# A hybrid decoder layer: gate operand sums made on chip, and rotary queries ahead of the GLA output halves

## The chip, the core and the metric

The kernel runs on one core of a Trainium2 chip. The metric is the time of one execution on the device in microseconds (us); before the change its median is 903.59 us over three runs (901.25 to 905.59). The core has five engines with a queue of instructions each: TensorE (PE) multiplies into PSUM, VectorE (DVE) and ScalarE (ACT) do elementwise work, GpSimd (POOL) does elementwise work in SBUF, and SyncE (SP) issues transfers. POOL and ACT issue some transfers too. An engine takes its queue in order.

## The reference

One layer of a decoder, 512 tokens of width 1024, in float32. A first LayerNorm gives h. From h one input projection makes the inputs of two branches: gated linear attention (GLA, four heads) and multi-head latent attention (MLA, eight heads, with a query latent of 384 and a key-value latent of 256). Two sets of gates are made from h as well and merge the branches; the output projection, a residual with LayerNorm, a squared-ReLU MLP of width 4096 and a last LayerNorm follow:

```python
h = layer_norm(x, ln_in_g, ln_in_b)
q_g, k_g, v_g, r_g, a_lr, q_lat, kv_lat, gate_logits = split(h @ w_in)
o_gla = rms_norm(gla_chunked(q_g, k_g, v_g, log_a))
y_gla = (o_gla * silu(r_g)) @ w_o_gla
q     = rms_norm(q_lat) @ w_q_b          # per head 128 plain and 64 rotary
kv    = rms_norm(kv_lat[:256]) @ w_kv_b  # per head 128 keys, 128 values
y_mla = merge_heads(causal_attention(q, rope(q), kv, k_rope)) @ w_o_mla
g_gla, g_mla = split(sigmoid(gate_logits + b_gate))
h = layer_norm(alpha * h + (g_gla * y_gla + g_mla * y_mla) @ w_out)
h = layer_norm(alpha * h + square(relu(h @ w_ff1)) @ w_ff2)
```

## The kernel before, in words

**Split numbers.** A float32 operand is kept as two parts, a high one rounded to the format that TensorE multiplies fast (`fp32r`) and a low one with the rest. A product takes three matmuls: high by high, high by low, low by high. `split` makes the parts: ScalarE copies (line 111 or 114), VectorE subtracts (112 or 115). Of h the kernel keeps only its two parts, eight tiles `hT` of 128 x 2 x 512 (feature rows by part by token).

**Weights.** All weights come through one stream, a list of entries in the order in which the plan calls stand in the code. `plan` appends entries of two 128-row blocks; `pump` (line 162 on) issues the loads on SP's queue up to two entries ahead and the splits (L185 on ACT, L186 on DVE) one entry ahead. High and low parts have two buffers each, so the split of an entry waits until the entry two before it is used up. `gemm_fm` (feature rows out, L238 to L240) and `gemm_tm` (token rows out, L271 to L273) consume them; an entry of a 512-wide `gemm_fm` is 24 matmuls of 512 columns. Their accumulators come from a PSUM pool `mm` of four banks; a second pool `px` of four banks serves the attention work.

**Stages around the change.** The *head* (0 to about 45 us) loads x, normalises it and transposes it into hT (`ln_transpose`, L406 to L420), one half of the tokens after the other, while the latent projections run. It also stores the unsplit h, tile by tile in halves of 256 tokens, from POOL's queue into DRAM tiles `hrawd` (L420). Then come the GLA projections with the GLA level work of each head woven between (`gla_levels`, `gla_out`; L657 to L800). The *first half of the gates* is two plain `gemm_fm` of hT (loop over `mb`). The *second half* is a Strassen-like product (`gemm_unit`, L1000 on): seven half-size products named in `FMO` in the order 11, 21, t1, 22, t2, t3, t4, whose h-side operands include four sums and differences of quarter blocks of h. A generator `op_sums` makes these during the first half of the gates: it loads two row blocks of raw h from `hrawd` into a tile `hraw` (L970, SP, prefetched up to two pairs ahead), forms four combinations `X` on VectorE (L974 to L977), and splits them (`sh`).

After the gates stand, in this order: output half 0 of the GLA branch (`y_gla(0)`), the rotary queries of heads 0 to 3 (`mla_qr(0)`), projections and attention of heads 0 and 1 (`mla_pair(0)`), output half 1 of GLA (`y_gla(1)`), the rotary queries of heads 4 to 7 (`mla_qr(1)`), and the other three pairs of heads. `mla_qr` multiplies the query latents `qlT` (three tiles `latT`) by the rotary columns of `w_q_b`, four token blocks of 256 columns in two PSUM banks, then applies the rotation (L487 to L489 on DVE, L490 on POOL), scales and splits (L114, L115), and spawns a generator that transposes the result (L821) into `QS`. The latents had been stored to DRAM (L541) and are loaded again (L1080) by the function `after`, which runs behind each of the seven products.

**What sets the order.** Generators (GLA heads, attention heads, transposes, `h_sums`) are advanced by `tick`, called between the matmul groups of a running product, so the program's text is already a weave. The kernel is then built with a scheduler that, on a timeline of its own at build time, gives each engine the earliest ready instruction in program order; what comes out is a fixed order per engine. Tiles come from pools with fixed counts (24 buffers of tag A for most, 22 of tag B), and an instruction that needs a buffer waits for its release.

Of the kernel before, what the change touches and what calls it, by code (L numbers as in the profile page):

```python
# [10 lines left out]
F32 = mybir.dt.float32  # L11
# [5 lines left out]
ALU = mybir.AluOpType  # L17
AX = mybir.AxisListType

P = 128  # L20
T = 512
# [31 lines left out]
def tile_hybrid_block(ctx: ExitStack, tc: tile.TileContext, I, out, dbg=None):  # L53
    nc = tc.nc
# [18 lines left out]
    def A(shape, dt=F32, n="a"):  # L73
        tag, bufs = ("C", 8) if n in TAG_C else (n, TAG_W[n]) if n in TAG_W else ("A", 24)
        return pa.tile(shape, dt, tag=tag, bufs=bufs, name=nm(n))
# [7 lines left out]
    def DR(shape, n):  # L83
        n = nm(n)
        return pd.tile(shape, F32, tag=n, name=n)
# [7 lines left out]
    def f(ap):  # L93
        return ap.bitcast(F32)

    act = nc.scalar.activation
    vtt = nc.vector.tensor_tensor
# [45 lines left out]
    def plan(name, c0, n, k_lo=0, k_hi=None, heads=None, res=False, per=2):  # L143
        w = I[name]
        K = w.shape[0] // P
        k_hi = K if k_hi is None else k_hi
        idx = []
        for k0 in range(k_lo, k_hi, per):
            nk = min(per, k_hi - k0)
            if heads is None:  # L150
                src = w.rearrange("(k p) n -> p k n", p=P)
                dmas = [(slice(0, nk), src[:, k0:k0 + nk, c0:c0 + n], None)]
            else:
                hw, h0, nh = heads
                src = w.rearrange("(k p) (h c) -> p k h c", p=P, c=hw)
                cw = n // nh
                dmas = [(kk, src[:, k0 + kk, h0:h0 + nh, c0:c0 + cw], cw) for kk in range(nk)]
            idx.append(len(stream))
            stream.append({"dmas": dmas, "nk": nk, "n": n, "res": res})
        return {"idx": idx, "nk": k_hi - k_lo, "per": per}  # L160
# [64 lines left out]
    def part(x, i, c):  # L225
        return x[i][:, c] if isinstance(x, tuple) else x[:, i, c]
# [72 lines left out]
    def plan_qr(g):  # L299
        PL["qr", g] = plan("w_q_b", NOPE, 4 * ROPE, heads=(HQ, 4 * g, 4))  # L300
# [26 lines left out]
    for key in UNITS:  # L327
        PL[key] = []
        for op, _ in FMO:
            for hf in range(2):  # L330
                PL[key].append(len(stream))
                e = {"nk": 2, "n": T, "res": False}
                if op[0] != "t":
                    e["dmas"] = [(slice(0, 2), u_src(key, int(op[0]) - 1, int(op[1]) - 1, hf), None)]
                else:
                    e["src"] = lambda q=(key, (op, hf)): WQ[q]
                if op == "22":
                    e["post"] = lambda raw, q=(key, "t1", "t2", hf): u_sum(*q, raw)
                elif op == "t2":
                    e["post"] = lambda raw, q=(key, "t2", "t4", hf): u_sum(*q, WQ[key, ("21", q[3])])  # L340
                stream.append(e)
    PL["yg", 0] = plan("w_o_gla", 0, T)
    plan_qr(0)

    def plan_pair(pr):
        PL["qn", pr] = plan("w_q_b", 0, 2 * P, heads=(HQ, 2 * pr, 2))
        PL["kn", pr] = plan("w_kv_b", 0, 2 * P, heads=(2 * P, 2 * pr, 2))
        PL["mv", pr] = plan("w_kv_b", P, 2 * P, heads=(2 * P, 2 * pr, 2))

    plan_pair(0)  # L350
    PL["yg", 1] = plan("w_o_gla", T, T)
    plan_qr(1)
    plan_pair(1)
    plan_pair(2)
    plan_pair(3)
# [43 lines left out]
    def ln_transpose(rows, g, b, outs, hf, alt=False, n="h0"):  # L399
        tk = slice(hf * 256, (hf + 1) * 256)  # L400
        for k in range(NK):
            if len(outs) <= k:
                outs.append(A([P, 2, T], F32R, n) if n == "h0" else (B([P, T], F32R, n), B([P, T], F32R, n)))
            p = MM() if alt and k in (4, 5) else PX()
            for i in range(2):
                nc.tensor.transpose(p[:, i * P:(i + 1) * P], rows[2 * hf + i][:, k * P:(k + 1) * P], ident)  # L406
            tmp = B([P, 256], F32, "lnt")
            hi, lo = part(outs[k], 0, tk), part(outs[k], 1, tk)
            ha = act(hi, p[:, :256], AF.Identity, scale=g[:, k:k + 1], bias=b[:, k:k + 1])
            if alt and k % 2:  # L410
                act(tmp, p[:, :256], AF.Identity, scale=g[:, k:k + 1], bias=b[:, k:k + 1])
            else:
                vts(tmp, p[:, :256], g[:, k:k + 1], b[:, k:k + 1], op0=ALU.mult, op1=ALU.add)
            hd = vtt(lo, tmp, f(hi), op=ALU.subtract)
            if n == "h1":
                st["ln"] = (ha, hd)
            else:
                if len(rawd) <= k:
                    rawd.append(DR([P, T], "hrawd"))
                nc.gpsimd.dma_start(rawd[k][:, tk], tmp)  # L420
            yield hd

    mvin = consts.tile([P, NT, 2], F32, name="mvin")
    hT, rawd = [], []

    def ln_in0():
        for tt in range(2):
# [87 lines left out]
    qlT, ckT, qld, ckd, GL, KKs = [], [], [], [], [], []  # L515
# [286 lines left out]
    def mla_qr(g):  # L802
        qst = []

        def ev_qr(a, j, ps):
            src = ps[:, :4 * ROPE].rearrange("p (h c) -> p h c", c=ROPE)
            csb = cs2[:, a, None, :].to_broadcast([P, 4, ROPE])
            snb = sn2[:, a, None, :].to_broadcast([P, 4, ROPE])
            t1 = B([P, 4, ROPE], F32, "rt1")
            t2 = B([P, 4, ROPE], F32, "rt2")  # L810
            rope(src, csb, snb, t1, t1, t2)
            q2 = B([P, 4, 2, ROPE], F32R, "q2")
            split(t1, q2[:, :, 0, :], q2[:, :, 1, :], scale=scale)
            qst.append(q2)
        gemm_tm([PL["qr", g]], qlT, 4 * ROPE, ev_qr)

        def tr():
            for h in range(4):
                p = PX(dt=F32R)
                for tt in range(NT):  # L820
                    nc.tensor.transpose(p[:, tt * P:(tt + 1) * P], qst[tt][:, h].rearrange("p a b -> p (a b)"), identr)  # L821
                yield
                q = B([P, T], F32R, "QS")
                act(q, f(p), AF.Copy)
                QS[4 * g + h] = q
        return spawn(tr())
# [134 lines left out]
    t_gla = [t_lv, t_out]  # L961


    def op_sums(srcs, rest, new, ops):
        raws = []
        for p in range(4):
            while len(raws) < min(4, p + 2):
                raws.append(A([P, 2, T], F32, "hraw"))
                for i in range(2):
                    nc.sync.dma_start(raws[-1][:, i], rest[2 * len(raws) - 2 + i])  # L970
            raw = raws[p]
            a11, a12, a21, a22 = raw[:, 0, :256], raw[:, 1, :256], raw[:, 0, 256:], raw[:, 1, 256:]
            X = A([P, 4, 256], F32, "hx")
            vtt(X[:, 0], a21, a22, op=ALU.subtract)  # L974
            vtt(X[:, 1], X[:, 0], a11, op=ALU.subtract)
            vtt(X[:, 2], a12, X[:, 1], op=ALU.add)
            vtt(X[:, 3], a11, a21, op=ALU.subtract)  # L977
            yield
            o = {0: (0, 0), 1: (1, 0), 4: (1, 1)}
            o = {ph: tuple(part(srcs[2 * p + i], w, slice(256 * h, 256 * h + 256)) for w in range(2))  # L980
                 for ph, (i, h) in o.items()}
            xs = new()
            for i in range(2):
                xh, xl = xs[i]
                split(X[:, 2 * i:2 * i + 2], xh, xl)
                o[(2, 5)[i]], o[(3, 6)[i]] = (xh[:, 0], xl[:, 0]), (xh[:, 1], xl[:, 1])
            yield
            ops.append(o)
# [8 lines left out]
    def gemm_unit(key, ops, evac, after=None):  # L997
# [3 lines left out]
        for n, (op, ph) in enumerate(FMO):  # L1001
# [43 lines left out]
            if after:  # L1045
                after(op)
# [13 lines left out]
    hops = []  # L1060

    def h_sums():
        yield from op_sums(hT, rawd,
                           lambda: [[B([P, 2, 256], F32R, "sh") for _ in range(2)] for _ in range(2)], hops)

    t_h = spawn(h_sums())
# [5 lines left out]
    def after(op):  # L1072
        if op == "11":
            u_load("g1", "t3")
            u_load("g1", "21")
        if op == "t4":
            for outs, rest in ((qlT, qld), (ckT, ckd)):
                for d in rest:
                    outs.append(A([P, 2, T], F32R, "latT"))
                    nc.sync.dma_start(f(outs[-1]), d)  # L1080
    gemm_unit("g1", hops, ev_gate, after)
    hT = hops = None


    def y_gla(mb):
        def ev_y(a, ps):
            g = gt[mb * 4 + a]
            stt(g[:, 0, :], g[:, 0, :], 1.0, ps, op0=ALU.add, op1=ALU.mult)
        gemm_fm(PL["yg", mb], ogT, T, ev_y)
# [17 lines left out]
            return omT[h]  # L1107
    omT_lazy = Lazy()

    WID[0] = 2  # L1110
    y_gla(0)
    mla_qr(0)
    WID[0] = 4
    t0, mv = mla_pair(0)
    mv()
    y_gla(1)
    mla_qr(1)
    t1, mv = mla_pair(1)
    mv(lambda: finish(*t0))
    t2, mv = mla_pair(2)  # L1120
# [283 lines left out]
```

## Time and profile before

| | |
|---|---|
| median of three runs | 903.59 us (901.25 to 905.59) |
| profiled execution | 902.01 us, span 900.2 us |
| granted TensorE clock | 0.998 |
| busy: TensorE, VectorE, ScalarE, GpSimd | 880.5, 580.5, 426.9, 181.1 us |
| transferred | 111.47 MB, mean 124 GB/s |

The profile is of one execution. "Busy" of TensorE counts matmuls from start to end, and neighbours overlap, so full busy time doesn't mean peak speed. A row of a group gives line, engine, operation, tiles (out<-in) and shapes, the number of instructions, and then busy time and mean duration or, in the view of a tile, the shortest, median and longest duration in ns and the first and last start in us. A row of the timeline begins with start and duration in us; what is in square brackets is the idle time of that engine just before it and what ended it. `xN` behind a row of the timeline stands for N like instructions in a row.

### The profile page before, as it was taken

The numbers are of one execution on the slowest core, as the hardware profiler recorded it, in microseconds if no ns is written. First come the engines' busy times: TensorE is split into PE (matmuls) and PEld (weight loads), VectorE is DVE, ScalarE is ACT, GpSimd is POOL, SyncE is SP. The second block draws the span as 40 slices with busy tenths as digits, with TensorE's granted clock in tenths as the row PEclk, the third lists the DMA queues.
The fourth block names the chain that finished last, engine by engine and source line by source line (L and its number), as shares of the span: only waits on it lengthen the run. The fifth ranks groups of instructions, "written<-read, shape, count | busy, mean of one in ns | idle before, by whom it ended". The sixth has DMA issues, their size and how long they took to land.

```text
span 900.2 us, 12222 instructions
## 1 busy us (share of the span) xinstructions
PE 880.5 (98%) x4652; PEld 755.2 (84%) x4652; DVE 580.5 (64%) x945; ACT 426.9 (47%) x729; POOL 181.1 (20%) x212
## 2 busy tenths in 40 slices
PE   5999999999999999999999999999999999999996
PEld 5988888888889988888888888988888888888885
DVE  7834855577956626576856797997557646723565
ACT  5556443444546524446644423366367546733410
POOL 3203442443511001010000002104400520142200
PEclk9999999999999999999999999999999999999999
DMA  7614423217326624112207618005941990494421
GB/s 260 198 47 156 129 67 94 71 47 215 113 71 211 188 59 126 27 54 65 82 24 271 197 47 304 1 0 151 296 115 32 260 246 24 116 204 110 132 67 74
DMA packets 66699, 111.47 MB, mean 124 GB/s; under 512 B 8225, under 2 KB 28065, under 8 KB 66641
## 3 DMA queue, kind: packets, MB, share of 16 engines
q1 hardware_dynamic: 52496, 77.67, 27.5%
q0 software_dynamic: 12224, 29.37, 13.7%
q10 hardware_dynamic: 1920, 3.66, 1.2%
q8 instruction: 36, 0.59, 0.3%
q14 instruction: 23, 0.18, 0.1%
HBM read 91.28 MB, written 6.82 MB: 109 GB/s over the span
## 4 chain that ended last, share of the span: by engine, by line
PE 95%; DVE 2%; DMA 2%; ACT 1%; issue 0%; SPq 0%; DVEq 0%; POOL 0%; ACTq 0%
PE mm L238 14%; PE mm L239 14%; PE mm L240 14%; PE mm L271 7%; PE mm L273 7%; PE mm L272 7%; PE px L1275 2%; PE px L1274 2%; PE px L1273 2%; PE px L727 2%; PE mm L1275 2%; PE mm L1274 2%; PE mm L1273 2%; PE mm L1023 1%; PE mm L1021 1%; PE mm L1022 1%
## 5 line engine op out<-in xcount | busy, mean ns | idle before, releaser
L186 DVE TENSOR_TENSOR wlo<-wraw,whi 128x1024 fp32r<-128x1024 f32 (+1 forms) x102 | 115.5, 1133 | 145.1 <-ACT whi L185 141.0
L185 ACT ACTIVATE whi<-wraw 128x1024 fp32r<-128x1024 f32 (+1 forms) x102 | 98.2, 963 | 123.0 <-PE mm L239 68.3
L238 PE MATMUL mm<-h,whi 128*128 128x512 f32 x352 | 137.4, 391 | 0.0
L239 PE MATMUL mm<-h,whi 128*128 128x512 f32 x352 | 137.2, 390 | 0.0
L240 PE MATMUL mm<-h,wlo 128*128 128x512 f32 x352 | 131.3, 390 | 0.0
L1287 POOL DMA_DIRECT2D res<-ev x48 | 41.7, 1006 | 189.0 <-ACT ev L1285 153.5
L238 PEld LDWEIGHTS mm<-h,whi 128*128 128x128 f32 x352 | 66.1, 188 | 13.6 <-ACT gt L1054 0.2
L239 PEld LDWEIGHTS mm<-h,whi 128*128 128x128 f32 x352 | 66.1, 188 | 13.4
L240 PEld LDWEIGHTS mm<-h,wlo 128*128 128x128 f32 x352 | 66.0, 188 | 13.4
L272 PE MATMUL mm<-wlo,h 128*128 128x512 f32 x128 | 50.3, 393 | 0.0
L273 PE MATMUL mm<-whi,h 128*128 128x512 f32 x128 | 50.1, 392 | 0.0
L271 PE MATMUL mm<-whi,h 128*128 128x512 f32 x128 | 49.7, 403 | 0.0
L185 ACT ACTIVATE xh<-wraw 128x1024 fp32r<-128x1024 f32 (+1 forms) x28 | 27.2, 985 | 39.1 <-PE mm L273 15.8
L666 POOL TENSOR_TENSOR rp<-rp 128x256 f32<-128x256 f32 x32 | 30.3, 946 | 64.2 <-ACT E L671 47.2
L1301 ACT ACTIVATE relu<-mm 128x512 f32<-128x512 f32 x32 | 18.8, 595 | 49.5 <-PE mm L240 49.3
L186 DVE TENSOR_TENSOR wlo<-wq,whi 128x1024 fp32r<-128x1024 f32 x20 | 24.5, 1224 | 24.9 <-ACT whi L185 24.9
L186 DVE TENSOR_TENSOR xl<-wraw,xh 128x1024 fp32r<-128x1024 f32 (+1 forms) x28 | 31.2, 1128 | 10.8 <-ACT xh L185 10.8
L673 DVE TENSOR_TENSOR M<-E,qk 128x512 f32<-128x512 f32 x32 | 27.3, 854 | 14.9 <-ACT E L671 14.9
L391 POOL TENSOR_TENSOR mv<-mv,mhalf 128x1 f32<-128x1 f32 x4 | 4.6, 1156 | 146.7 <-DVE mv L390 146.7
L671 ACT ACTIVATE E<-rp 128x512 f32<-128x512 f32 x32 | 20.4, 637 | 25.6 <-POOL rp L667 25.6
L667 POOL TENSOR_TENSOR rp<-rp 128x256 f32<-128x256 f32 x32 | 28.8, 900 | 7.9 <-ACT q L696 5.7
L273 PEld LDWEIGHTS mm<-whi,h 128*128 128x128 f32 x128 | 24.0, 188 | 5.0
(405 smaller groups left out, 2412.1 us busy)
## 6 DMA issues: line engine op xcount, KB each, us to landing
wraw<-in_w_ff_dram SPq DMA_DIRECT2D x40, 512.0 KB, 4.9
wraw<-in_w_in_dram SPq DMA_DIRECT2D x38, 512.0 KB, 3.6
wq<-in_w_ff_dram POOLq DMA_DIRECT2D x24, 512.0 KB, 8.9
res<-ev POOLq DMA_DIRECT2D x48, 256.0 KB, 6.7
wraw<-in_w_o_gla_dram SPq DMA_DIRECT2D x8, 512.0 KB, 4.0
wraw<-in_w_o_mla_dram SPq DMA_DIRECT2D x8, 512.0 KB, 3.6
wraw<-in_w_out_dram SPq DMA_DIRECT2D x8, 512.0 KB, 4.2
wq<-in_w_in_dram SPq DMA_DIRECT2D x6, 512.0 KB, 5.8
```

The lines of the kernel that those rows point to most:

```text
L185: st["ins"] = act(hi[:, :nk, :n], raw[:, :nk, :n], AF.Copy)
L186: vtt(lo[:, :nk, :n], raw[:, :nk, :n], f(hi[:, :nk, :n]), op=ALU.subtract)
L238: mm(o, hi[:, c], xh, start=first, stop=False)
L239: mm(o, hi[:, c], xl, start=False, stop=False)
L240: mm(o, lo[:, c], xh, start=False, stop=last)
L271: mm(o, xh, hi[:, :n], start=opens, stop=False, skip_group_check=share)
L272: mm(o, xh, lo[:, :n], start=False, stop=False, skip_group_check=share)
L273: mm(o, xl, hi[:, :n], start=False, stop=last, skip_group_check=share)
L1273: mm(o, xh[:, c], hi[:, pp], start=opens, stop=False, skip_group_check=True)
L1274: mm(o, xh[:, c], lo[:, pp], start=False, stop=False, skip_group_check=True)
L1275: mm(o, xl[:, c], hi[:, pp], start=False, stop=hf == 1 and pp == 1, skip_group_check=True)
L1287: nc.gpsimd.dma_start(res[tt + t][:, j * T:(j + 1) * T], e, accum_op=ALU.add)
```

## The change

Two things. First, the raw h is no longer stored in the head and loaded again for the gates: `op_sums` forms it on VectorE as the sum of its two parts, one addition of 128 x 512 for each of the eight blocks, one more step of the generator for each of the four pairs. Second, the rotary queries of each group stand ahead of the GLA output half that they followed: queries 0 directly behind the gates, queries 1 directly behind the value projection of the first pair, both in the plan of the weights and in the code that consumes them. With that, the three query latents are loaded again behind the product t2 and only the two key-value latents behind t4.

```diff
+    plan_qr(0)
     PL["yg", 0] = plan("w_o_gla", 0, T)
-    plan_qr(0)
...
     plan_pair(0)
+    plan_qr(1)
     PL["yg", 1] = plan("w_o_gla", T, T)
-    plan_qr(1)
...
             if n == "h1":
                 st["ln"] = (ha, hd)
-            else:
-                if len(rawd) <= k:
-                    rawd.append(DR([P, T], "hrawd"))
-                nc.gpsimd.dma_start(rawd[k][:, tk], tmp)
...
-    def op_sums(srcs, rest, new, ops):
-        raws = []
+    def op_sums(srcs, new, ops):
         for p in range(4):
-            while len(raws) < min(4, p + 2):
-                raws.append(A([P, 2, T], F32, "hraw"))
-                for i in range(2):
-                    nc.sync.dma_start(raws[-1][:, i], rest[2 * len(raws) - 2 + i])
-            raw = raws[p]
+            raw = A([P, 2, T], F32, "hraw")
+            for i in range(2):
+                h = srcs[2 * p + i]
+                vtt(raw[:, i], f(part(h, 0, slice(0, T))), f(part(h, 1, slice(0, T))), op=ALU.add)
+            yield
...
-        if op == "t4":
-            for outs, rest in ((qlT, qld), (ckT, ckd)):
+        if op in ("t2", "t4"):
+            for outs, rest in {"t2": ((qlT, qld),), "t4": ((ckT, ckd),)}[op]:
                 for d in rest:
                     outs.append(A([P, 2, T], F32R, "latT"))
                     nc.sync.dma_start(f(outs[-1]), d)
...
+    mla_qr(0)
     WID[0] = 2
     y_gla(0)
-    mla_qr(0)
     WID[0] = 4
     t0, mv = mla_pair(0)
     mv()
+    mla_qr(1)
     y_gla(1)
-    mla_qr(1)
```

More of the change, by code (lines that the diff above doesn't have):

```diff
@@ L416, in ln_transpose @@
                 st["ln"] = (ha, hd)
-            else:
-                if len(rawd) <= k:
-                    rawd.append(DR([P, T], "hrawd"))
-                nc.gpsimd.dma_start(rawd[k][:, tk], tmp)
             yield hd
     mvin = consts.tile([P, NT, 2], F32, name="mvin")
-    hT, rawd = [], []
+    hT = []
     def ln_in0():
@@ L1062, in h_sums @@
     def h_sums():
-        yield from op_sums(hT, rawd,
+        yield from op_sums(hT,
                            lambda: [[B([P, 2, 256], F32R, "sh") for _ in range(2)] for _ in range(2)], hops)
```

## The prediction

> **What bounds the kernel now.** I read the page first, then the waits of TensorE alone, then a table of windows. Of the page four lines matter:
>
> ```profile
> span 900.2 us, 12222 instructions
> PE 880.5 (98%) x4652; PEld 755.2 (84%) x4652; DVE 580.5 (64%) x945; ACT 426.9 (47%) x729; POOL 181.1 (20%) x212
> PEclk9999999999999999999999999999999999999999
> PE 95%; DVE 2%; DMA 2%; ACT 1%; issue 0%; SPq 0%; DVEq 0%; POOL 0%; ACTq 0%
> ```
>
> TensorE is busy for 880.5 of 900.2 us at a granted clock in the top tenth throughout, and the chain that ended last runs through it for 95% of the span. So the question is only where the other 19.7 us lie and which of them the change can reach. All waits of TensorE that the profile shows (who waited, for whom; us, times, longest):
>
> ```profile
> PE px L406 <- ACT x L395: 9.1, 1, 9.1
> PE px L860 <- DVE PT L112: 0.7, 1, 0.7
> PE mm L238 <- DVE qn L115: 0.6, 1, 0.6
> PE px L406 <- DVE lnt L413: 0.5, 1, 0.5
> PE mm L1023 <- DVE wlo L186: 0.5, 1, 0.5
> PE mm L271 <- ACT lat L502: 0.4, 1, 0.4
> PE mm L238 <- ACT h L409: 0.3, 1, 0.3
> ```
>
> The first, 9.1 us, is the start: x is loaded and normalised before there is anything to multiply. The six others sum to 3.0 us. The rest, 19.7 - 9.1 - 3.0 = 7.6 us, is the last LayerNorm at the end. Neither end is touched by the change. Here is its neighbourhood by windows (busy us of PE, PEld, DVE, ACT, POOL, then clock, DMA share, GB/s):
>
> ```profile
> 20.00:40.00 20.00, 19.64 (x125) 18.93 (x124) 17.75 (x43) 10.40 (x17) 5.43 (x10) 1.00 0.83 272
> 200.00:220.00 20.00, 20.00 (x110) 16.77 (x109) 15.32 (x30) 10.22 (x18) 9.65 (x11) 1.00 0.59 187
> 220.00:240.00 20.00, 20.00 (x111) 17.50 (x109) 16.04 (x27) 9.18 (x19) 8.32 (x9) 1.00 0.61 172
> 240.00:260.00 20.00, 19.97 (x114) 16.72 (x113) 17.64 (x28) 11.77 (x20) 8.94 (x10) 1.00 0.18 53
> 260.00:280.00 20.00, 20.00 (x123) 17.94 (x123) 6.75 (x10) 9.35 (x18) 1.02 (x1) 1.00 0.30 80
> 340.00:360.00 20.00, 19.38 (x120) 17.04 (x120) 12.74 (x27) 9.74 (x18) 3.10 (x4) 1.00 0.48 142
> ```
>
> TensorE is full where the sums are made (200 to 260) and loses 0.6 us where the rotary queries stand (340 to 360). The matmul count is unchanged, so the change can gain at most those 3.0 us of waits, 0.33%, and it can lose whatever new wait it makes. About 0.5% (4.5 us) is what a measurement of this kernel can tell from no change. A caution on "busy": a 512-column matmul shows 0.39 us, but the next starts 0.23 us after it:
>
> ```profile
> 338.41 0.39 PE L238 MATMUL mm<-ogT,whi 128*128 128x512 f32 x1
> 338.64 0.39 PE L239 MATMUL mm<-ogT,whi 128*128 128x512 f32 x1
> ```
>
> I reckon matmul work at 0.23 us each; a wait shorter than 0.16 us would not show as idle.
>
> **The change part by part. The stores in the head.** Sixteen stores of 128 KB from POOL's queue go:
>
> ```profile
> 13.52 2.89 POOL L420 DMA_DIRECT2D hrawd<-lnt  x5 [4.08 <-DVE lnt L413]
> 36.61 1.60 POOL L420 DMA_DIRECT2D hrawd<-lnt  x3 [1.01 <-DVE lnt L413]
> hrawd<-lnt POOLq DMA_DIRECT2D x16, 128.0 KB, 5.0
> 22.00:26.00 4.00, 4.00 (x28) 3.98 (x27) 2.99 (x7) 1.48 (x3) 0.55 (x1) 1.00 1.03 363
> 30.00:34.00 4.00, 3.64 (x23) 3.26 (x22) 3.86 (x9) 3.20 (x6) 1.11 (x2) 1.00 0.91 269
> ```
>
> POOL loses 16 x 0.54 = 8.6 us of issuing, and the DMA engines 2.1 MB of traffic where they are full (share 1.03 at 22 to 26). But TensorE, at 4.00 of 4.00 there, isn't waiting for a load. The waits in this stage that come after the first store are those for lat (0.4, the 0.36 us missing at 30 to 34) and for h (0.3). ScalarE, whose copies free lat and make h, also starts weight splits that wait for loads, so a quicker load can shorten these two: between 0 and 0.7 us. Both are late evacuations, not late loads, so I take 0.3. Next late there would be VectorE, at 3.86 of 4.00. POOL's small LayerNorm operations behind the stores wait for VectorE already and gain nothing.
>
> **The sums.** Eight loads of 256 KB on SP's queue and their 2 MB go, and eight VectorE additions of 128x512 come. The rows of what stands there now, of a like addition, of the split that follows the sums, and of their first consumer:
>
> ```profile
> L970 SPq DMA_DIRECT2D hraw<-hrawd x8: 335/440/799, 211.7 to 219.6; - x8
> L977 DVE TENSOR_TENSOR hx<-hraw x4: 411/414/1076, 218.6 to 248.8; 128x256 f32<-128x256 f32 x4
> L673 DVE TENSOR_TENSOR M<-E,qk x32: 676/693/1160, 101.0 to 256.0; 128x512 f32<-128x512 f32 x32
> L112 DVE TENSOR_TENSOR sh<-hx,sh x8: 677/896/1218, 227.8 to 253.1; 128x512 fp32r<-128x512 f32 x8
> L1021 PE MATMUL mm<-sh,whi x64: 278/283/385, 287.6 to 310.4; 128*128 128x256 f32 x64
> ```
>
> One costs 0.693 us, so eight cost 5.5 us; at the slowest of the same form, 1.160, they cost 9.3 us. The operand, hT, has been whole since the head, so they never block VectorE's queue by waiting. They stand beside gate matmuls. The last operand made from the sums is ready by 253.1 + 1.2 = 254.3, and the first is used at 287.6, with 13.25 us of idle VectorE between 260 and 280: delay of the sums alone costs nothing. What is queued behind them on VectorE are the low halves of the gate weights (L186) and the last GLA levels:
>
> ```profile
> 268.41 1.05 ACT L185 ACTIVATE whi<-wraw 128x1024 fp32r<-128x1024 f32 x1
> 269.49 1.22 DVE L186 TENSOR_TENSOR wlo<-wraw,whi 128x1024 fp32r<-128x1024 f32 x1 [6.78 <-ACT whi L185]
> ```
>
> A split takes 1.05 + 1.22 = 2.3 us and must be done within one weight entry of 24 matmuls, 24 x 0.23 = 5.5 us: 3.2 us of cover, more where GLA matmuls lie between. I take 0; the upper end is 9.3 - 3.2 = 6.1 us, the whole addition arriving as one delay. SP's queue loses eight issues of about 0.44 us; its loads there are ahead of need, so no gain.
>
> That column prices contention. The 128x256 form takes 0.41 or, at worst, 1.08 us, and POOL is 42 to 48% busy in those windows. The Trainium skill ("SBUF — State Buffer", section "Who interferes with whom") says that a VectorE instruction with two SBUF inputs and a GpSimd instruction that reads SBUF exclude each other for the whole instruction. By that every added sum, having two SBUF inputs, could wait and could hold up POOL's GLA additions; the sum by the rule is the 9.3 us end, and by the median row the 5.5.
>
> **The latents' reload.** Three of five loads (512 KB each, SP) move from behind the last product to two products earlier:
>
> ```profile
> L1080 SPq DMA_DIRECT2D latT<-latd x5: 320/338/467, 283.3 to 307.4; - x5
> DMA to landing us min/median/max: 3.1/3.8/9.2
> 317.31 0.40 PE L238 MATMUL mm<-ogT,whi 128*128 128x512 f32 x1
> 339.09 0.28 PE L271 MATMUL mm<-whi,latT 128*128 128x256 f32 x1
> 343.29 0.28 PE L273 MATMUL mm<-whi,latT 128*128 128x256 f32 x1
> 351.34 0.27 DVE L489 TENSOR_TENSOR rt<-mm,sn 128x128 f32<-128x128 f32 x1
> 350.35 0.50 PE L238 MATMUL mm<-latT,whi 128*128 128x512 f32 x1 [0.62 <-DVE qn L115]
> ```
>
> The rotary queries will read them at about 317.3 (where the gate unit ends) instead of 339.1. Already now the last of the five is issued at 307.4; the three query latents come first. Even 9.2 us after 307.4 is 316.6, in time. Behind them on SP wait the query weights, three loads of 128 KB for the first products, small; cost 0, upper end 0.6.
>
> **The two moves.** Rotary queries 0 (36 matmuls of 256 columns, 339.09 to 343.29, 4.2 us) go ahead of GLA output half 0, queries 1 ahead of half 1. TensorE's work is the same. Today the 0.62 us wait at 350.35 comes from this place: VectorE works off rotary products (to 351.34 + 0.27 = 351.6), weight splits and the following projection in one queue, and the projection finds its PSUM not free. With half 0 behind the queries, that wait goes: -0.6. Late next is the PSUM of half 0. It wants four accumulators of a pool of four; two come free with the last gate evacuations, and the queries hold the other two until VectorE has read them. Today the last read is 351.6, 8.2 us after the queries' last matmuls at 343.4. With three accumulators TensorE has 18 matmuls per entry and two entries split ahead, 36 x 0.23 = 8.3 us: it just reaches. At the lower end no wait; with two accumulators only, 24 x 0.23 = 5.5 and 8.2 - 5.5 = 2.7 us. I take half of today's wait, 0.3, at each of the two places (at the second the value projection's two banks, drained early, play the gates' part): +0.6, between 0 and 5.4. The transposes of the rotary queries then stand inside half 0 and half 1, 16 each as before. POOL's four rotary additions per group move too, into a queue that is idle at 320.
>
> **The sum.** -0.3 (head) + 0 (sums) + 0 (reload) - 0.6 + 0.6 (moves) = -0.3 us on the profiled execution's 902.01 (span 900.2 and 1.81 around it): 901.7. The median of the runs, 903.59, lies 1.58 above that execution; 903.3 on the median.
>
> **The rivals.** *VectorE falls behind in the gates (slower).* VectorE is busy 15.32 + 16.04 + 17.64 = 49.0 of 60 us from 200 to 260. With 5.5 more it is at 54.5, with 9.3 at 58.3. Its idle time is made of waits for ScalarE and can't all be filled. If the low halves come later than the 3.2 us of cover, TensorE waits: at 9.3 us, +6.1, and nothing of that comes back, since TensorE has no slack to make it up. 903.6 + 6.1 - 0.3 = 909.4; it decides against "no change" from a delay of about 8 us. For it: the 17.64 of 20. Against: the additions can be done at any time before 280, and no wait on wlo over 0.5 us shows today. *PSUM after the rotary queries:* both half-outputs start with two accumulators: 903.6 + 5.4 - 0.9 = 908.1. For it: 8.2 against 8.3; against: behind the queries no projection's evacuation shares VectorE, and the rotary reads come sooner than 8.2. *All shown waits go:* 903.6 - 3.0 = 900.6, still within 0.5%. Against it: the waits for PT, for wlo and for lnt belong to steps that the change leaves as they are. *The moves change nothing:* the program is ordered by readiness when it is built, so what follows may simply be fetched from another place; 903.6, and my number hardly differs.
>
> **How the numbers follow.** My sum: 0.55. The moves change nothing: 0.15. All shown waits go: 0.07. VectorE later than the cover: 0.10, of which 0.07 reach over 0.5%. PSUM: 0.08, of which 0.06 do. The 0.05 left are a gain of over 0.5%: it needs more than all the waits that are shown, so an effect that isn't in them, or a lucky order of the rebuilt program. Together faster 0.05, same 0.55 + 0.15 + 0.07 + 0.03 + 0.02 = 0.82, slower 0.13. The range goes from 900.6 (all waits gone) to 908.1 (the PSUM rival), leaving out about 1 in 20 on each side.
>
> **What would show it.** Right: no hraw loads, eight new 128x512 additions of some 0.7 us between 205 and 270, no wait of TensorE on wlo of the gates, and TensorE's waits without the 9.1 sum to 2 to 4 us. The first step is wrong if TensorE's idle time at 13 to 45 falls by more than 0.7 us; the second if VectorE in 240 to 260 is at 20 and TensorE waits on wlo; the moves' step if TensorE waits on rt or q of the rotary queries, or for latT at about 317. The number as a whole is wrong if the order that is built around the gates loses a wait of several us that no row of now foreshadows.

## The result

Over 22 executions of each kernel, the changed one takes 901.53 us in the median (900.38 to 902.65) and the one before 902.15 us (901.23 to 905.83). The ratio is 0.9983, with a 95% interval of 0.9975 to 0.9992: faster by 0.17%, and within the 0.5% that the chances went by. A good part of that ratio isn't in the typical execution: 8 of the 22 executions of before lie at 903.6 to 905.8 us, a group of their own ("upper runs"), and none of the changed kernel does.

The page of the changed kernel, its first lines:

```profile
span 900.2 us, 12161 instructions
PE 880.9 (98%) x4652; PEld 755.8 (84%) x4652; DVE 585.5 (65%) x953; ACT 427.3 (47%) x729; POOL 178.0 (20%) x196
```

The matmuls are the same 4652. VectorE has eight instructions and 5.0 us more, POOL sixteen issues fewer. The waits of TensorE in the changed kernel (who for whom; us, times, longest):

```profile
PE px L406 <- ACT x L395: 9.5, 1, 9.5
PE px L723 <- DVE SD L679: 0.5, 1, 0.5
PE mm L240 <- DVE wlo L186: 0.5, 1, 0.5
PE mm L1018 <- DVE wlo L186: 0.5, 1, 0.5
PE mm L238 <- ACT h L409: 0.3, 1, 0.3
PE px L406 <- DVE lnt L413: 0.2, 1, 0.2
```

Without the start they sum to 2.0 us, against 3.0 before. Gone are the waits for qn, PT and lat, and the one for lnt is 0.3 shorter; new are one for SD (a masked copy of the GLA levels) and one for the low half of a weight entry on L240, the GLA output half. By stage (busy us of PE, PEld, DVE, ACT, POOL, then clock, DMA share, GB/s), changed kernel:

```profile
20.00:40.00 20.00, 20.00 (x129) 19.72 (x128) 17.71 (x42) 11.14 (x18) 2.59 (x2) 1.00 0.58 173
240.00:260.00 20.00, 19.42 (x117) 16.26 (x116) 19.89 (x35) 11.51 (x19) 10.82 (x10) 1.00 0.19 53
260.00:280.00 20.00, 20.00 (x121) 17.91 (x120) 7.39 (x12) 9.77 (x19) 2.60 (x2) 1.00 0.34 104
320.00:340.00 20.00, 19.49 (x104) 16.04 (x104) 10.17 (x20) 7.86 (x12) 3.88 (x4) 1.00 0.26 78
340.00:360.00 20.00, 20.00 (x114) 17.45 (x113) 10.85 (x22) 7.27 (x18) 0.00 (x0) 1.00 0.38 111
420.00:440.00 20.00, 20.00 (x124) 17.35 (x123) 14.47 (x35) 11.27 (x29) 0.00 (x0) 1.00 0.31 103
```

and the last window of the kernel before:

```profile
420.00:440.00 20.00, 19.34 (x117) 16.45 (x116) 14.46 (x34) 11.48 (x29) 0.00 (x0) 1.00 0.29 92
```

TensorE's idle time against before: -0.36 us at 20 to 40, +0.55 at 240 to 260 (where VectorE is now full, 19.89 of 20), +0.51 at 320 to 340, -0.62 at 340 to 360, -0.66 at 420 to 440. The start varies by some tenths between executions, so one length to compare is from the start of the first matmul to that of the last. The timeline of TensorE has them, and between them the first matmul of the GLA projections, where the head ends; changed kernel first, then the kernel before:

```profile
9.47 0.90 PE L406 MATMUL px<-ca,x 128*128 128x128 f32 x3 [9.47 <-ACT x L395]
47.87 0.40 PE L238 MATMUL mm<-h,whi 128*128 128x512 f32 x1
892.26 0.28 PE L1345 MATMUL mm<-xh,hid 128*128 128x256 f32 x1
```

```profile
9.11 1.11 PE L406 MATMUL px<-ca,x 128*128 128x128 f32 x4 [9.11 <-ACT x L395]
47.93 0.40 PE L238 MATMUL mm<-h,whi 128*128 128x512 f32 x1
892.33 0.28 PE L1350 MATMUL mm<-xh,hid 128*128 128x256 f32 x1
```

892.26 - 9.47 = 882.79 against 892.33 - 9.11 = 883.22: -0.43 us. All of that lies in the head. Behind it, from the first GLA matmul to the last matmul, it is 892.26 - 47.87 = 844.39 against 892.33 - 47.93 = 844.40 us: no difference. The head is no steady measure. In four profiles of one and the same kernel ("moves only" below) it takes 38.36 to 39.28 us from the first matmul to the first GLA matmul, while the rest takes 843.75 to 844.02. So two single executions that differ by 0.4 us from first to last show no gain yet; what a step of the change does is better read behind the head.

The profiled executions take 901.97 and 902.01 us. The 14 executions of before that are not upper runs have a mean of 901.84 us, the 22 of the changed kernel one of 901.51. So the typical gain is 0.3 us, and the remaining 1.2 of the 1.5 us that the ratio stands for (0.17% of 902) come from the upper runs that are missing.

The sums and the last operand made from them, in the changed kernel:

```profile
L965 DVE TENSOR_TENSOR hraw<-h x8: 677/702/1105, 215.5 to 251.2; 128x512 f32<-128x512 f32 x8
L112 DVE TENSOR_TENSOR sh<-hx,sh x8: 676/684/1128, 234.2 to 272.7; 128x512 fp32r<-128x512 f32 x8
```

And the new wait on L240, by VectorE's timeline with ScalarE's high half of the same entry (its timeline) above it:

```profile
320.98 1.06 ACT L185 ACTIVATE whi<-wraw 128x1024 fp32r<-128x1024 f32 x1 [1.85 <-PE mm L273]
```

```profile
321.82 0.42 DVE L483 TENSOR_TENSOR rt<-mm,cs 128x256 f32<-128x256 f32 x1 [2.96 <-PE mm L273]
322.16 0.28 DVE L484 TENSOR_TENSOR rt<-mm,sn 128x128 f32<-128x128 f32 x1
322.36 0.28 DVE L485 TENSOR_TENSOR rt<-mm,sn 128x128 f32<-128x128 f32 x1
322.55 2.89 DVE L186 TENSOR_TENSOR wlo<-wraw,whi 128x1024 fp32r<-128x1024 f32 x2
```

The high half is done at 322.04, but VectorE's queue has the first rotary product ahead of the low half. That product waits 2.96 us for a query matmul (L273), so the low half starts at 322.55, 0.5 us late, and TensorE waits as long for it.

### The profile page after: what moved, and what is told of

The parts are those of the page before. It is cut to its first block, busy times and chain, and to the rows that moved or that the text cites. A ratio compares the mean times of both kernels' runs of the same rounds, so it can differ in the third digit from the quotient of the medians.

```text
span 900.2 us, 12161 instructions
## 1 busy us (share of the span) xinstructions
PE 880.9 (98%) x4652; PEld 755.8 (84%) x4652; DVE 585.5 (65%) x953; ACT 427.3 (47%) x729; POOL 178.0 (20%) x196
## 4 chain that ended last, share of the span: by engine, by line
PE 96%; DVE 2%; DMA 1%; ACT 1%; issue 0%; SPq 0%; DVEq 0%
PE mm L238 14%; PE mm L240 14%; PE mm L239 14%; PE mm L271 7%; PE mm L273 7%; PE mm L272 7%; PE px L1269 2%; PE px L1270 2%; PE px L1268 2%; PE px L723 2%; PE mm L1269 2%; PE mm L1270 2%; PE mm L1268 2%; PE mm L1018 1%; PE mm L1016 1%; PE mm L1017 1%
## 5 line engine op out<-in xcount | busy, mean ns | idle before, releaser
L240 PE MATMUL mm<-h,wlo 128*128 128x512 f32 x352 | 130.5, 390 | 0.0
L240 PEld LDWEIGHTS mm<-h,wlo 128*128 128x128 f32 x352 | 66.0, 188 | 13.5
L273 PE MATMUL mm<-whi,h 128*128 128x512 f32 x128 | 50.1, 392 | 0.0
L273 PEld LDWEIGHTS mm<-whi,h 128*128 128x128 f32 x128 | 24.0, 188 | 5.0
```

The source lines that it names most:

```text
L240: mm(o, lo[:, c], xh, start=False, stop=last)
L273: mm(o, xl, hi[:, :n], start=False, stop=last, skip_group_check=share)
```

## The experiments

The times of all kernels that were run, with the ratio to the kernel before, measured beside it on the same chip. "First to last" is the start of the last matmul less that of the first, and "behind the head" the start of the last matmul less that of the first GLA matmul, both in the profiled execution, in us.

| kernel | median (range), us | n | ratio [95%] | first to last | behind the head |
|---|---|---|---|---|---|
| before | 902.15 (901.23 to 905.83) | 22 | 1 | 883.22 | 844.40 |
| changed | 901.53 (900.38 to 902.65) | 22 | 0.9983 [0.9975, 0.9992] | 882.79 | 844.39 |
| sums only | 902.18 (901.65 to 902.69) | 12 | 0.9998 [0.9990, 1.0006] | 883.38 | 845.05 |
| moves only | 902.85 (900.93 to 907.24) | 12 | 1.0005 [0.9991, 1.0019] | 882.71 | 844.02 |
| stores kept | 902.10 (901.40 to 902.65) | 12 | 0.9998 [0.9989, 1.0006] | 883.45 | 844.41 |
| sums thrice | 907.78 (906.17 to 908.32) | 6 | 1.0058 [1.0044, 1.0072] | 889.07 | 850.56 |
| query weights in one entry | 900.80 (900.61 to 901.43) | 12 | 0.9975 [0.9966, 0.9985] | 882.16 | 843.55 |
| sums later | 901.06 (900.66 to 903.04) | 12 | 0.9981 [0.9970, 0.9991] | 884.35 | 845.55 |
| both of these | 900.17 (899.79 to 900.41) | 6 | 0.9967 [0.9954, 0.9979] | 881.43 | 843.04 |
| loads back, waited for | 902.23 (901.38 to 902.70) | 11 | 1.0002 [0.9993, 1.0011] | 883.30 | 844.71 |
| loads back, unread | 903.70 (902.75 to 905.16) | 11 | 1.0021 [1.0012, 1.0030] | 884.02 | 845.44 |

The kernel before ran again beside each group, and how many of its executions lay above 903.5 us differs: 8 of 22 beside the changed kernel, 5 of 29 beside the next four kernels, 12 of 30 beside the three after them, 1 of 20 beside the last two. So ratios of different groups don't compare to a tenth of a percent.

**One part at a time.** The first kernel has the sums and no stores, with the order of before:

```diff
-                nc.gpsimd.dma_start(rawd[k][:, tk], tmp)
...
-                    nc.sync.dma_start(raws[-1][:, i], rest[2 * len(raws) - 2 + i])
...
+                vtt(raw[:, i], f(part(h, 0, slice(0, T))), f(part(h, 1, slice(0, T))), op=ALU.add)
```

> The kernel before with the first part of the change alone: no stores in the head, sums on VectorE, rotary queries and reload where they were. Theory A (the difference is the sum of TensorE's waits by place): head -0.4 us (TensorE's wait for lat gone), gates +0.6 (wait for SD behind the sums), the waits for qn (0.6) and PT (0.7) stay: +0.2 us, ratio 1.000. Theory B (the stores cause the upper runs of before, 904 to 906 us): no run above 903, ratio 0.998. Theory C (all of the gain is in the moves): ratio 1.000 to 1.001, and upper runs remain.

Its waits, those that matter here:

```profile
PE px L856 <- DVE PT L112: 0.7, 1, 0.7
PE mm L238 <- DVE qn L115: 0.6, 1, 0.6
PE px L723 <- DVE SD L679: 0.5, 1, 0.5
```

The wait for SD is here, and those for qn and PT have stayed: Theory A by place. Behind the head it is 845.05 - 844.40 = +0.65 us, the price of the sums; from first to last it is +0.16, as this execution's head is 0.49 shorter, and the ratio is 0.9998. None of the 12 executions is an upper run, as Theory B wants, but the stores are not the only thing that this kernel lacks; it lacks the loads too.

The second kernel has the moves and the earlier reload alone:

```diff
+    plan_qr(0)
     PL["yg", 0] = plan("w_o_gla", 0, T)
-    plan_qr(0)
...
+    mla_qr(0)
     y_gla(0)
-    mla_qr(0)
```

> The kernel before with the second part alone: rotary queries ahead of the output halves and the earlier reload, with the stores and the loads of raw h kept. Theory A: wait for qn gone (-0.6), a wait for wlo behind the rotary products (+0.5 to 0.7), wait for PT gone (-0.7 to -1.0), head as before: -0.9 us, ratio 0.999. Theory B: the upper runs of before are here too, ratio 1.000. Theory C: ratio 0.998.

Windows of this kernel:

```profile
20.00:40.00 20.00, 19.98 (x126) 19.18 (x125) 17.32 (x42) 10.44 (x17) 5.43 (x10) 1.00 0.82 268
320.00:340.00 20.00, 19.49 (x102) 15.90 (x101) 10.17 (x20) 7.87 (x12) 3.87 (x4) 1.00 0.28 81
420.00:440.00 20.00, 20.00 (x122) 17.27 (x121) 14.31 (x36) 10.88 (x29) 0.00 (x0) 1.00 0.29 95
```

The new wait at 320 to 340 (0.51) is here, and the waits for qn and PT are gone: both belong to the moves. Behind the head it is 844.02 - 844.40 = -0.38 us. TensorE has a wait of 0.25 us for SD there, which the three later profiles of this kernel, further down, don't have: they have 843.75 to 843.79, or -0.61 to -0.65. That is less than the -0.9 of Theory A. Its median is nevertheless the worst of the three, since half of its executions are upper ones: 6 of 12 above 902.8 us (the count of 7 in a later expectation is a slip). So behind the head the two parts act by place independently and cancel: +0.65 for the sums, about -0.63 for the moves, and -0.01 for the whole change. What a typical execution gains, 0.3 us, isn't behind the head in these profiles, and where it comes from isn't shown.

Third, the changed kernel with the stores put back and nothing that reads them:

> The changed kernel, but the sixteen stores of the head stay, though nothing reads them. What this tells is the price of the stores alone. Theory A: +0.4 us on the changed kernel, the wait for lat in the head is back, ratio to before 0.9988. Theory B: the upper runs (904 to 906) are back, ratio 1.000. Theory C: as the changed kernel, 0.998.

```profile
20.00:40.00 20.00, 19.96 (x125) 19.18 (x125) 17.08 (x40) 10.51 (x18) 5.43 (x10) 1.00 0.85 271
```

No upper run in 12 speaks against Theory B, the stores as their cause, though before itself had only 5 in 29 beside it, and at that rate 12 without one come about one time in ten. The time of 902.10 can't be held against the 902.18 of the sums-only kernel: 2.5 us of it lie outside the span (902.65 with a span of 900.1 in the profiled execution), against 1.8 there (902.18 with 900.4). Behind the head it is as the changed kernel, 844.41. In the head TensorE loses 0.04 us at 20 to 40, where before lost 0.36 with the same stores. Over all profiles, a wait for lat shows in four of the eight with the stores (0.36, 0.16, 0.16 and 0.22 us) and in none of the six without them, while the head takes 38.36 to 39.28 us with them and 38.33 to 38.80 without. So the stores may cost a few tenths; these profiles don't separate that from what one kernel varies by.

**How much more VectorE could take.** The additions three times over:

```diff
-                vtt(raw[:, i], f(part(h, 0, slice(0, T))), f(part(h, 1, slice(0, T))), op=ALU.add)
+                for _ in range(3):
+                    vtt(raw[:, i], f(part(h, 0, slice(0, T))), f(part(h, 1, slice(0, T))), op=ALU.add)
```

> The changed kernel with each of the eight additions made three times: 16 more of 0.70 us, 11 us more of VectorE between 215 and 270, where VectorE is busy 19.89 of 20 us from 240 to 260 in the changed kernel. If VectorE's cover in the gates is used up by the change (the slow rival of the prediction was near): TensorE waits for wlo of the gates or for SD, +2 to +6 us, ratio 1.001 to 1.005. If the idle 12.6 us of VectorE between 260 and 280 take it up: within 0.5 us of the changed kernel, 0.998 to 0.999.

TensorE's waits without the start, three windows, and the additions of this kernel:

```profile
PE px L786 <- DVE og L780: 2.6, 1, 2.6
PE mm L1019 <- DVE wlo L186: 1.8, 2, 1.3
PE px L723 <- DVE SD L679: 0.6, 1, 0.6
PE mm L240 <- DVE wlo L186: 0.5, 1, 0.5
PE mm L238 <- ACT h L409: 0.3, 1, 0.3
```

```profile
280.00:284.00 4.00, 1.36 (x11) 1.06 (x11) 2.37 (x5) 1.91 (x5) 1.02 (x1) 1.00 0.72 187
284.00:288.00 4.00, 4.00 (x22) 4.00 (x22) 0.59 (x2) 0.00 (x0) 0.67 (x1) 0.57 1.02 321
288.00:292.00 4.00, 4.00 (x35) 3.92 (x34) 2.01 (x3) 3.17 (x6) 1.76 (x2) 1.00 1.03 347
```

```profile
L966 DVE TENSOR_TENSOR hraw<-h x24: 673/679/1106, 214.7 to 261.3; 128x512 f32<-128x512 f32 x24
```

It is 907.78 us, 5.5 above before and 6.2 above the changed kernel, just over the +2 to +6 that was expected: the slow rival of the prediction is real, from some point between 5.6 and 16.3 us of additions (8 and 24 at 0.70 and 0.68). It doesn't come as predicted, though. The gate weights aren't late in the first half; the last GLA head's output is late (og), TensorE has nothing left at 281 to 283, and then the clock falls.

**The two new waits taken away.** First the query weights in one stream entry:

```diff
-        PL["qr", g] = plan("w_q_b", NOPE, 4 * ROPE, heads=(HQ, 4 * g, 4))
+        PL["qr", g] = plan("w_q_b", NOPE, 4 * ROPE, heads=(HQ, 4 * g, 4), per=3)
```

> The changed kernel with the rotary query weights of a group as one stream entry of three 128-row blocks instead of two entries, so that the split of the first weights of the output half finds a free buffer when the queries begin and no longer stands behind the first rotary product on VectorE. Theory A (the wait for wlo at about 323 comes from that): the wait of 0.5 (0.7 us by the starts of the matmuls) goes, 0.6 us less than the changed kernel, ratio to before 0.9978. Rival (the wait is PSUM or the rotary work itself): the wait stays or turns into one for the accumulators, 0.998.

VectorE's timeline of this kernel:

```profile
318.89 1.23 DVE L186 TENSOR_TENSOR wlo<-wraw,whi 128x1024 fp32r<-128x1024 f32 x1 [2.08 <-ACT whi L185]
321.54 0.42 DVE L483 TENSOR_TENSOR rt<-mm,cs 128x256 f32<-128x256 f32 x1 [1.43 <-PE mm L273]
```

The low half of the output's first weights is made at 318.89, before the rotary products, and TensorE no longer waits for it; first to last is 882.16, -0.63 us against the changed kernel, and behind the head 843.55, -0.84. Theory A holds and PSUM is ruled out, as nothing about the banks was changed.

Second the sums four steps later:

```diff
     def h_sums():
+        for _ in range(4):
+            yield
```

> The changed kernel with the sums four steps later in the gates, so that more of them fall between 260 and 280 where VectorE is idle 12.6 us. Theory A (the wait for SD at about 245 comes from the added VectorE work beside the last GLA levels): that wait goes, 0.5 us less than the changed kernel, ratio 0.9978; the sums are still ready before 287. Rival (the wait is due to the rebuilt order, not to the load): the wait stays, or another of the same size comes.

The median is 901.06, the wait for SD is gone. But the profiled execution is 903.04, the slowest of the twelve, and shows a part of why:

```profile
PE mm L1018 <- DVE wlo L186: 1.8, 2, 1.3
```

```profile
292.63 1.23 DVE L324 TENSOR_TENSOR wq<-wq,wraw 128x1024 f32<-128x1024 f32 x1 [2.03 <-DMA wraw<-in_w_in_dram]
```

In that execution a weight load of the gate unit landed late, VectorE stood 2.03 us for it with the next low half behind it in the queue, and TensorE waited 1.3 us. That is 1.3 of the 2.0 us that this execution lies above the median.

Both edits together:

> Both edits: the waits at 245 and at 323 go, about 1.1 us less than the changed kernel, ratio to before 0.997.

```profile
PE px L406 <- ACT x L395: 9.3, 1, 9.3
PE mm L1018 <- DVE wlo L186: 0.5, 1, 0.5
PE mm L238 <- ACT h L409: 0.3, 1, 0.3
PE px L406 <- DVE lnt L413: 0.2, 1, 0.2
```

```profile
260.00:280.00 20.00, 20.00 (x124) 17.92 (x123) 12.18 (x23) 11.16 (x22) 1.02 (x1) 1.00 0.21 56
```

```profile
9.28 1.11 PE L406 MATMUL px<-ca,x 128*128 128x128 f32 x4 [9.28 <-ACT x L395]
890.71 0.28 PE L1347 MATMUL mm<-xh,hid 128*128 128x256 f32 x1
```

Those are all of its TensorE waits, its window of 260 to 280, where VectorE's work has gone from 7.39 to 12.18 us, and, from the timeline, its first and last matmul. 890.71 - 9.28 = 881.43, -1.36 us against the changed kernel (-1.35 behind the head), and 900.17 us in the median: 0.9967 of before, better than both kernels. With the sums later, the wait for SD is gone in both kernels that have this edit.

**The upper runs.** The same moves-only kernel once more, for a profile of one of them:

> The moves-only kernel once more, for a profile of one of its upper runs (7 of 12 runs lay above 902.8 us, against none of 46 in the kernels without the loads of raw h). Theory D (the loads of raw h land late in such a run, and VectorE's queue stands until they do): the loads land after more than 12 us, VectorE waits for them over 4 us, and TensorE waits 1 to 4 us between 220 and 260, for wlo or SD. Rival E (the upper runs are late elsewhere, at the start or the end): 220 to 260 is as before, and the difference lies in the first 9 us or the last 8. If the profiled execution isn't an upper one, this stays open.

The profiled execution took 901.47 us and is not an upper one, though 4 of the 8 executions are (903.5 to 906.5). Two kernels then put the loads of raw h back into the changed kernel with the stores, one into the tiles that the sums write next, one into tiles that nothing reads (shown; the other has the tiles' name `hraw` and `raw = raws[p]` in place of the last line):

```diff
+        raws = []
         for p in range(4):
+            while len(raws) < min(4, p + 2):
+                raws.append(A([P, 2, T], F32, "hdum"))
+                for i in range(2):
+                    nc.sync.dma_start(raws[-1][:, i], rest[2 * len(raws) - 2 + i])
             raw = A([P, 2, T], F32, "hraw")
```

> The changed kernel with the stores kept and the loads of raw h put back into the tiles that the sums then overwrite, so VectorE waits for each landing though it needs nothing of it. Theory D (upper runs come of VectorE standing for a late load of raw h): a third to a half of the runs lie 2 to 4 us above the rest, as in before and in the moves-only kernel. Rival F (they come of the traffic alone, which makes weights late elsewhere): upper runs too, and equally in the next kernel, where nobody waits for these loads. Rival G (of neither, only of the order that was built): no upper runs.

> The changed kernel with the stores kept and the loads of raw h put back into tiles that nothing reads. Theory D: no upper runs, median as the kernel with the stores kept, 902.1. Rival F: upper runs as in the kernel where VectorE waits. Rival G: none in either.

None of the 11 executions was an upper one where the tiles are overwritten, and in the profile VectorE had no wait for these loads. Where the loads are unread, 4 of 11 were at 904.8 to 905.2, over a group at 902.8 to 903.8 that is itself higher; its profile shows

```profile
PE px L790 <- DVE SD L683: 1.3, 1, 1.3
```

a longer wait for SD. By these counts both theories miss: D wanted upper runs in the first of the two and none in the second, F wanted them in both. But beside these two kernels before itself had only 1 of 20 above 903.5 us, so the 11 without one tell little, and VectorE never stood for a load in the profile, which was D's condition. D isn't settled by this.

> A further profile of the moves-only kernel, half of whose runs are upper ones (10 of 20 above 902.8 us). In an upper run Theory D wants loads of raw h that land later than 12 us after issue and a wait of VectorE for them of over 4 us with TensorE waiting between 220 and 260; Rival F wants a wait for weights (wraw) instead.

> The same once more, since any single execution is an upper one in only about half of the cases: Theory D and Rival F expect what was said for the look before.

The executions that were profiled took 901.77 and 902.18 us, again none of the upper ones. What VectorE waits for the loads in the first moves-only profile, also a typical execution:

```profile
  DMA hraw<-hrawd: 2.6, 2
DMA to landing us min/median/max: 5.8/8.1/11.5
```

It stands 2.6 us for them, and this is the profile in which TensorE waits 0.25 us for SD; in the three later ones VectorE stands 0.5 to 1.2 us and TensorE has no such wait. What can be said: there were upper runs in three kernels, all of which load raw h from DRAM (before, moves only, loads unread), not in every kernel that does (none of 11 in loads waited for), and in none of the 64 executions of five kernels that don't load it (changed, sums only, stores kept, one entry, both), against 25 of 81 of before, measured beside them. The two others without the loads are sums thrice, all of whose 6 lie within 2.2 us, and sums later, with its one slow execution explained in part above. How they come about was not caught in a profile and stays open.

The clocks of the single executions hold a hint. Of the 23 above 904.4 us (before, moves only and loads unread), 18 have a mean granted clock of 0.993 to 0.996; no execution below 904.4 us has less than 0.997. A clock lower by 0.002 over 902 us is 1.8 us. In sums thrice a mean of 0.996 goes with one stretch of a lowered clock behind a long wait of TensorE (last section). So an upper execution may be one in which some wait grew long enough for the same; that is argued, not shown.

## Why the prediction was right, and where not

The time was given as 903.3 in 900.6 to 908.1, with 0.82 on "within 0.5%"; it is 901.53, within. That the change could gain no more than the 3.0 us of waits, and so not 0.5%, held, and that is what the chances rested on. The forecast difference was -0.3 us; typical executions differ by -0.3, the medians by -0.62, the ratio stands for -1.5. That the first of these agrees is luck: the sums, forecast as 0, cost 0.65 us behind the head, the moves, forecast as 0 together, gained about 0.63, and the two errors cancel. The 1.8 us between 903.3 and 901.53 come mostly from the base: the 903.59 to which the -0.3 was added is itself one of the upper runs, 1.44 above the median of 22. By its steps:

- *The stores, -0.3.* The wait for lat is gone and TensorE is full at 20 to 40. But two kernels that have the stores lose only 0.02 and 0.04 us there, where before lost 0.36, and the head's length varies by more than that; so the stores may cost a few tenths, and it isn't shown.
- *The sums, 0.* A wait of +0.5 us, +0.65 in all behind the head. The eight additions took 0.702 us in the median against 0.693 forecast, their last operand was ready by 272.7 + 1.1 and first used at 288, so delay of the sums themselves cost nothing, as said. The step that failed is what is queued behind them: not a gate weight with its 3.2 us of cover, but a masked copy of the GLA levels (SD), which has none. Sums only has the same wait; with the sums four steps later it is gone. Of the sign named for this step one half came, VectorE at 19.89 of 20; the wait was for SD and not for wlo.
- *The contention with GpSimd.* The additions are 677 at best and 1105 ns at worst, the median near the best, so the sum goes by the 5.5 us end. The Trainium skill ("SBUF — State Buffer", section "Who interferes with whom") has VectorE with two SBUF inputs and a GpSimd read exclude each other; the slowest of the eight would fit that, but no run here tells that cause from another. What the prediction said of GpSimd's side shows in a row of the changed kernel:

```profile
L741 POOL TENSOR_TENSOR sd<-SD,sd x4: 1284/1298/4339, 125.9 to 257.2; 128x512 fp32r<-128x512 f32 x4
```

The slowest, 4.34 us, is the last one, at 257.2, beside VectorE's work on the sums; before, all four took 1.28 to 1.30. Sums only, stores kept and sums thrice have it too (4.34 to 4.41), moves only doesn't. In the changed kernel TensorE has no wait for it.
- *The reload, 0.* Right: TensorE doesn't wait for latT in the changed kernel.
- *The moves, -0.6 and +0.3 and +0.3.* The wait for qn went, 0.62. In its place came 0.5 at the first output half, not 0.3, and for another reason: no PSUM bank, but the low half of the weights behind a waiting rotary product in VectorE's queue, which the query weights in one entry removes. At the second output half nothing came. And the wait for PT, which I had put among the steps that the change leaves as they are, went with the moves (-0.66; sums only keeps it, moves only has lost it). Together the moves gained about 0.63 us behind the head where 0 was forecast. Why PT's wait went is only argued: the queries of the second group no longer stand between the output half and the pair whose attention waited. In VectorE's timeline two weight splits (430.61 and 431.75) stand just ahead of the PT product at 432.36 before, one (431.24) ahead of that at 431.85 in the changed kernel.
- *The rivals.* "VectorE falls behind" didn't happen at 5.6 us of additions and did at 16.3. Its place was not the one named, and its price was too high: by its working 16.3 us would have cost 16.3 - 3.2 = 13.1, and the kernel is 6.2 us longer, a part of it through the clock. The PSUM rival didn't happen. "All shown waits go" is nearly what the last kernel reaches: 1.0 us of waits left.
- *What wasn't in the argument:* the upper runs. The three times shown (901.25 to 905.59) held two of them, 903.59 and 905.59, and I took the spread as noise around one middle.

## What to carry to other kernels

Where TensorE is busy for 98%, the list of its waits bounds what a rearrangement can win in a typical execution, and each wait has a place: kernels with one part of the change show it wait by wait. Compare from a matmul behind the start, where lengths repeat: here the head alone varied by 0.9 us between executions of one kernel. When work is added to an engine that is off the critical path, look at what has no cover in its queue right behind it, not at what has most of the busy time; and when a product is moved ahead of a weight's split, its evacuation may stand before that split and hold it while it waits for TensorE itself. A few upper executions can make more of a ratio than the typical one: look at the single times before explaining a median.

## What was not expected of the hardware

With the sums three times over, a single wait of 2.6 us cost more than its length. TensorE idles 2.64 of the 4 us from 280 to 284, and from 284 to 288 the granted clock is 0.57 and 22 matmuls are started, against 35 in the 4 us after, where the clock is 1.00 again, as it is in every window shown of the other kernels. The waits of that kernel without the start sum to 5.8 us (2.6, 1.8, 0.6, 0.5, 0.3) against 2.0 in the changed one, 3.8 more, yet behind the head it is 850.56 - 844.39 = 6.2 us longer. Four of its six executions have a mean clock of 0.996 (907.66 to 908.32 us), two 0.998 (906.17 and 906.95). The Trainium skill ("TensorE: Matmul & The Clock Gate", Part 1) tells of a clock that is halved after an idle window of about 3.4 us; here the drop followed an idle stretch of 2.64 us, shorter than that figure, and the measurement decides. Waits of 1.3 us, in the kernels with the sums later and with the unread loads, show no drop (0.998 in both profiled executions).
